# Moving the depthwise convolution of 128 channels from TensorE and VectorE to GpSimd, in the mixing layers of a two-block transformer on one Trainium2 core

## The chip, the core and the metric

The kernel runs on one core of one Trainium2 chip. The core has a matrix engine (TensorE, PE in the profile), three engines for elementwise work (VectorE or DVE, ScalarE or ACT, GpSimd or POOL) and a queue that issues transfers (SyncE, SP). Each engine takes its instructions strictly in the order in which they stand in its own queue. An instruction that has to wait for another engine holds up everything behind it in its queue.

The metric is device time in microseconds (us) for one execution of the whole program. Before the change the median of three runs is 1859.77 us.

## What is computed

Two blocks are run over 256 tokens of width 1024, all in float32. The first block has two layers of feed-forward, attention and feed-forward again. The second block has two layers, each a mixing layer and a feed-forward layer with a short convolution. The change touches only the mixing layers. Cut to what matters here, a mixing layer is:

```python
h = rms_norm_2(x, norm_mix_pre[l])
za, zq, zkv, zg, zc, zd = split(h @ w_in[l])
y_conv = conformer_conv(za, ...)     # 256 channels
y_nsa  = nsa_attention(zq, zkv, zg, ...)   # 4 heads, three branches
y_sgu  = spatial_gating(zc, ...)
y_pool = multiscale_pool(zd, ...)
y = concatenate([y_conv, y_nsa, y_sgu, y_pool], axis=-1) @ w_out[l]
x = x + rms_norm_2(y, norm_mix_post[l])

def conformer_conv(z, w, b, ln_g, ln_b):
    a, gate = split(z, 2, axis=-1)
    y = causal_dwconv(a * sigmoid(gate), w, b)   # 31 taps, one weight per channel and tap
    return silu(layer_norm(y, ln_g, ln_b))
```

The convolution is depthwise: each of the 256 channels is a sum of 31 shifted copies of itself, each multiplied with that channel's weight for the tap.

## The kernel before

Activations lie with channels on the 128 partitions and the 256 tokens along a row, so the 256 channels of the convolution are two tiles of 128x256 each. The gated input is `ci` (two tiles, each with 30 zeros ahead for the causal shift), the sums are `yc[0]` and `yc[1]`. All of these, with the attention's probabilities `PP` and their transposes `PT`, are parts of one large tile, `ar`, and carry that name in the profile.

Weights are streamed from HBM in chunks (`wraw`). Each unit of 128x1024 is split into a rounded part and a rest: ScalarE writes `whi`, VectorE writes `wlo` as `wraw` minus `whi`. A product of float32 accuracy then takes three matmuls, which the profile shows as `hh,whi`, `hl,whi`, `hh,wlo` (input side) or `oh,whi`, `ol,whi`, `oh,wlo` (output side, where `oh` and `ol` are the split result of the four parts). Such triples make up nearly all of TensorE's work.

`mix` (one call per layer) records the instructions. `begin` makes the first two column groups, whose outputs are gated by `gated_input` on ScalarE and VectorE. Then the column groups follow in the order of `MIX_ORDER`. Smaller pieces of work are Python generators that are advanced between the matmuls: `conv_gen`, `sgu_gen`, `pool_gen`, `nsa_cmp`, and `nsa_heads` once for each pair of heads. The second `nsa_heads` starts after the first has written its last product, since both use `PP` and `PT`. Last come the 192 matmuls with `w_out`, 48 for each of the four parts in the order of `MIX_ROWS`: spatial gating (2), pooling (3), convolution (0), attention (1). A part's matmuls are recorded when its result has been stored.

Where a generator's instructions land among the matmuls is decided when the program is built, by `Clock`: it adds up an estimated duration for every instruction on every engine, and `on(engine, ...)` lets a generator go on only when its inputs would be ready by then. An engine's prices are the functions handed to `Engine`. For GpSimd that price was 200 ns and 1 ns per column. VectorE's taps of the convolution are a filler: `conv_gen` records them when VectorE is estimated to be less than 1000 ns (`CONV_BEHIND`) behind TensorE, and `fill_gap` when VectorE would sit idle over 400 ns.

The convolution is divided like this. `yc[0]` is 31 taps on VectorE: one `TENSOR_SCALAR` and 30 `SCALAR_TENSOR_TENSOR`, each of which multiplies and adds in one instruction. Of `yc[1]`, the first 18 taps (`NDIAG`) are matmuls in float32 with a diagonal matrix each, `conv` in `MIX_ORDER`, and the other 13 are on VectorE, with one more addition that joins the two. The 18 diagonal matrices are made by ScalarE in `mix_ahead`, during the feed-forward layer before. Then `conv_gen` transposes both sums on TensorE, takes mean and variance on VectorE (`bs`, `mv`, `rs`, `rz`), normalises (`cz`), transposes back, applies Silu on ScalarE (`cs`) and splits into `oh` and `ol`.

Of the kernel before, what the change touches and what calls it, by code (L numbers as in the profile page):

```python
# [32 lines left out]
S = 256  # L33
# [23 lines left out]
MIX_ORDER = 'v u conv cvf kk cw1 q cvt zd'.split()  # L57
# [10 lines left out]
def _weights(seg):  # L68
# [34 lines left out]
    elif kind == "mix":  # L103
        for which in ["ag0", "ag1"] + [w for w in MIX_ORDER if w != "conv"]:
            n = 1 if which in ("cvf", "kk") else 2
            out.append((("cw1", l) if which == "cw1" else ("mixt" if which in ("v", "cvt", "zd") else "mix", l, which), n))
# [270 lines left out]
NDIAG = 18  # L377
# [55 lines left out]
class Clock:  # L433
# [6 lines left out]
    def __init__(self, nc):  # L440
# [25 lines left out]
        self.gpsimd = Engine(nc.gpsimd, self, "pool", lambda op, out, *a: 200 + size(out))  # L466
# [198 lines left out]
class K:  # L665
# [1103 lines left out]
    def conv_gen(self, l, ci, ready, y, products):  # L1769

        nc = self.nc
        taps = [0, NDIAG]

        def tap():
            t = int(ready[1] and taps[1] <= taps[0])
            if taps[t] == 31:
                t = 1 - t
            if taps[t] == 31 or t and not ready[1]:
                return False
            j = taps[t]  # L1780
            taps[t] += 1
            w = self.v("cw", (l * 2 + t) * 31 + j)
            if j == t * NDIAG:
                nc.vector.tensor_scalar(y[t], ci[:, t, j:j + S], w, self.v("cb", l * 2 + t),
                                        op0=OP.mult, op1=OP.add)
            else:
                nc.vector.scalar_tensor_tensor(y[t], ci[:, t, j:j + S], w, y[t], op0=OP.mult, op1=OP.add)
            return True

        while min(taps) < 31:  # L1790
# [251 lines left out]
    def mix_ahead(self, l):  # L2042
# [22 lines left out]
        self.diags = [self.ar[:, AR - 128 * i - 128:AR - 128 * i] for i in range(NDIAG)]  # L2065
        for j, d in enumerate(self.diags):
            yield from self.on("act", out=[d])
            nc.scalar.activation(d, self.c("ident"), AF.Copy, scale=self.v("cw", (l * 2 + 1) * 31 + j))
            yield
        self.there = l  # L2070

    def mix(self, l, norm, following):
# [14 lines left out]
        assert AR - 128 * NDIAG >= self.ar_at - 2687  # L2087
# [18 lines left out]
        def gated_input(t, ps):  # L2106
# [8 lines left out]
            if t == 0:  # L2115
                self.fillers.append(store(self.conv_gen(l, ci, gated, yc, convp), 0))
# [4 lines left out]
        convp = []  # L2121

        def conv_products():

            self.wait(lambda: gated[1])
            ps = self.mm()
# [198 lines left out]
```

## Time and profile before

| | |
|---|---|
| median of three runs | 1859.77 us (1859.73 to 1861.74) |
| the profiled execution | 1859.25 us, of which its span is 1857.5 us |
| PE busy | 1791.3 us (96%) |
| VectorE busy | 1478.0 us (80%) |
| ScalarE busy | 1006.7 us (54%) |
| GpSimd busy | 42.8 us (2%), 51 instructions |
| first mixing layer | from about 1226 to 1331 us of the span |
| second mixing layer | from about 1544 to 1649 us of the span |

Busy time on PE is the sum of matmuls that overlap in a pipeline, so 96% says that the engine seldom stands still and not that it is at its peak. The two mixing layers run the same program and make up some 11% of the span; everything that the change removes or adds, but for the diagonal matrices, lies in them. Within a mixing layer the profile is read by stretches, since its first part (the column groups) and its second (the two pairs of heads, one after the other) wait for different things. Nearly every row has the same source line, that of the helper which records instructions, so instructions are told apart by the names of their tiles.

### The profile page before, as it was taken

The numbers are of one execution on the slowest core, as the hardware profiler recorded it, in microseconds if no ns is written. First come the engines' busy times: TensorE is split into PE (matmuls) and PEld (weight loads), VectorE is DVE, ScalarE is ACT, GpSimd is POOL, SyncE is SP. The second block draws the span as 40 slices with busy tenths as digits, with TensorE's granted clock in tenths as the row PEclk, the third lists the DMA queues.
The fourth block names the chain that finished last, engine by engine and source line by source line (L and its number), as shares of the span: only waits on it lengthen the run. The fifth ranks groups of instructions, "written<-read, shape, count | busy, mean of one in ns | idle before, by whom it ended". The sixth has DMA issues, their size and how long they took to land.

```text
span 1857.5 us, 36497 instructions
## 1 busy us (share of the span) xinstructions
PE 1791.3 (96%) x15134; PEld 1749.9 (94%) x15134; DVE 1478.0 (80%) x2694; ACT 1006.7 (54%) x1705; POOL 42.8 (2%) x51
## 2 busy tenths in 40 slices
PE   6999999999999999999999999999899999999997
PEld 6999998999999999999999899998799998889997
DVE  6978798898779867779788865589698879869876
ACT  3534568544454445555565654454676554567653
POOL 0200010000000000000000000000000000000000
PEclk9999999999999999999999999999999999999999
DMA  9799374499849873533433566533256533325550
GB/s 383 308 342 341 125 294 184 144 367 351 316 151 345 338 272 134 182 137 123 145 119 137 205 246 221 187 130 137 92 198 215 185 146 136 114 78 206 216 182 24
DMA packets 54471, 378.86 MB, mean 204 GB/s; under 512 B 6304, under 2 KB 7808, under 8 KB 9376
## 3 DMA queue, kind: packets, MB, share of 16 engines
q1 hardware_dynamic: 52992, 372.94, 54.3%
q0 software_dynamic: 1168, 3.46, 0.6%
q8 instruction: 118, 1.93, 0.4%
q14 instruction: 49, 0.40, 0.1%
q10 hardware_dynamic: 144, 0.13, 0.0%
HBM read 375.41 MB, written 1.05 MB: 203 GB/s over the span
## 4 chain that ended last, share of the span: by engine, by line
PE 69%; issue 18%; DVE 7%; ACT 5%; POOL 1%; DMA 0%; POOLq 0%; SPq 0%; DVEq 0%; ACTq 0%
PE banks L427 69%; DVE wlo L427 2%; DVE ar L427 2%; ACT ar L427 2%; ACT whi L427 1%; POOL rz L427 1%; DVE x L427 1%; ACT L427 1%; ACT hh L427 1%; DVE sq L427 0%; DVE hl L427 0%; DMA x<-x 0%; ACT sq L427 0%; DVE ht L427 0%; DVE rs L427 0%
## 5 line engine op out<-in xcount | busy, mean ns | idle before, releaser
L427 DVE TENSOR_TENSOR wlo<-wraw,whi 128x1024 fp32r<-128x1024 f32 x557 | 669.7, 1220 | 172.2 <-ACT whi L427 171.2
L427 PE MATMUL banks<-hh,whi 128*128 128x256 f32 (+1 forms) x2792 | 796.2, 285 | 7.6 <-ACT hh L427 4.7
L427 PE MATMUL banks<-hh,wlo 128*128 128x256 f32 (+1 forms) x2792 | 786.1, 282 | 2.2 <-DVE wlo L427 2.2
L427 PE MATMUL banks<-hl,whi 128*128 128x256 f32 (+1 forms) x2792 | 786.2, 282 | 0.2
L427 ACT CAST whi<-wraw 128x1024 fp32r<-128x1024 f32 x557 | 569.6, 1048 | 172.2 <-DMA wraw<-w 85.1
L427 PEld LDWEIGHTS banks<-hh,whi 128*128 128x128 f32 x2792 | 529.3, 190 | 11.2 <-ACT hh L427 5.6
L427 PEld LDWEIGHTS banks<-hh,wlo 128*128 128x128 f32 x2792 | 529.2, 190 | 2.9 <-DVE wlo L427 2.9
L427 PEld LDWEIGHTS banks<-hl,whi 128*128 128x128 f32 x2792 | 530.0, 190 | 1.1 <-DVE hl L427 1.1
L427 PE MATMUL banks<-oh,whi 128*128 128x256 f32 x1312 | 373.1, 284 | 9.1 <-ACT oh L427 4.3
L427 PE MATMUL banks<-ol,whi 128*128 128x256 f32 x1312 | 368.7, 281 | 4.0 <-DVE ol L427 3.8
L427 PE MATMUL banks<-oh,wlo 128*128 128x256 f32 x1312 | 368.1, 281 | 0.0
L427 PEld LDWEIGHTS banks<-oh,whi 128*128 128x128 f32 x1312 | 247.6, 189 | 16.9 <-ACT oh L427 5.6
L427 PEld LDWEIGHTS banks<-ol,whi 128*128 128x128 f32 x1312 | 247.8, 189 | 4.9 <-DVE ol L427 4.9
L427 PEld LDWEIGHTS banks<-oh,wlo 128*128 128x128 f32 x1312 | 247.7, 189 | 0.0
L427 DVE CUSTOM_DVE_ANT_0 wraw<-wraw,cb 128x1024 f32<-128x1024 f32 x128 | 152.0, 1216 | 0.4 <-DMA wraw<-w 0.4
L427 ACT ACTIVATE sg<-banks 128x256 f32<-128x256 f32 x82 | 31.4, 384 | 176.2 <-PE banks L427 176.1
L427 PE MATMUL banks<-whi,hh 128*128 128x256 f32 x352 | 103.0, 293 | 1.6 <-ACT hh L427 1.4
L427 PE MATMUL banks<-whi,hl 128*128 128x256 f32 x352 | 99.6, 283 | 0.0
L427 PE MATMUL banks<-wlo,hh 128*128 128x256 f32 x352 | 99.3, 282 | 0.0
L427 DVE SCALAR_TENSOR_TENSOR cy<-cs,vec,cy 128x255 f32<-128x255 f32 (+1 forms) x176 | 83.6, 480 | 7.8 <-ACT cy L427 4.7
L427 DVE TENSOR_TENSOR sg<-banks,sg 128x256 f32<-128x256 f32 x82 | 34.4, 422 | 66.1 <-ACT sg L427 66.1
L427 ACT ACTIVATE cy<-cs,vec 128x256 f32<-128x256 f32 x88 | 47.9, 594 | 49.6 <-DVE cs L427 48.8
(207 smaller groups left out, 1698.8 us busy)
## 6 DMA issues: line engine op xcount, KB each, us to landing
wraw<-w SPq DMA_DIRECT2D x342, 1024.0 KB, 4.9
ar<-w SPq DMA_DIRECT2D x8, 1024.0 KB, 10.5
wraw<-w SPq DMA_DIRECT2D x5, 512.0 KB, 3.2
ar<-lw POOLq DMA_DIRECT2D x2, 752.0 KB, 4.8
x<-x SPq DMA_DIRECT2D x1, 1024.0 KB, 6.6
out<-x SPq DMA_DIRECT2D x8, 128.0 KB, 1.9
ar<-bands POOLq DMA_DIRECT2D x1, 544.0 KB, 8.3
cb<-c SPq DMA_DIRECT2D x1, 512.0 KB, 4.5
```

Of the source, the lines that this page charges most:

```text
L427: return f(out, *args, **kw)
```

## The change

The second 128 channels are summed on GpSimd alone. For each tap GpSimd multiplies the shifted row into one half of a new tile `ctmp`, and adds that half to `yc[1]`: 31 multiplications (the first adds the bias and writes `yc[1]` itself) and 30 additions of 128x256 for each layer. The 18 matmuls, VectorE's 13 taps and its joining addition go, and so do the diagonal matrices. A zeroing of 128x960 columns (`blk`, read by `cvf`) goes from GpSimd to VectorE. GpSimd's price in `Clock` is raised to 200 ns and 1.5 ns per column, 2.1 for an operation on two tensors. `conv_gen` waits for a third entry in `gated`, which is appended when the last addition has been recorded. The core of the diff:

```diff
-MIX_ORDER = 'v u conv cvf kk cw1 q cvt zd'.split()
+MIX_ORDER = 'v u cvf kk cw1 q cvt zd'.split()
...
-        self.gpsimd = Engine(nc.gpsimd, self, "pool", lambda op, out, *a: 200 + size(out))
+        self.gpsimd = Engine(nc.gpsimd, self, "pool", lambda op, out, *a: 200 + (2.1 if op == "tensor_tensor" else 1.5) * size(out))
...
-        while not products:
+        while len(ready) < 3:
             yield
-        yield from self.on("dve", products[0])
-        nc.vector.tensor_tensor(y[1], y[1], products[0][:, :S], op=OP.add)
-        self.rel(products[0])
         yield from self.on("pe", *y)
...
-        self.diags = [self.ar[:, AR - 128 * i - 128:AR - 128 * i] for i in range(NDIAG)]
-        for j, d in enumerate(self.diags):
-            yield from self.on("act", out=[d])
-            nc.scalar.activation(d, self.c("ident"), AF.Copy, scale=self.v("cw", (l * 2 + 1) * 31 + j))
-            yield
...
+        tmp = v3(self.qkt("ctmp"))
 
         def conv_products():
 
-            self.wait(lambda: gated[1])
-            ps = self.mm()
-            for j, d in enumerate(self.diags):
-                nc.tensor.matmul(ps[:, :S], d, ci[:, 1, j:j + S], start=j == 0, stop=j == NDIAG - 1)
-                if j % 3 == 2:
-                    self.step()
-            convp.append(ps)
-
+            for j in range(31):
+                while not gated[1] or nc.behind("pool") > CONV_BEHIND:
+                    yield
+                src, w = ci[:, 1, j:j + S], self.v("cw", (l * 2 + 1) * 31 + j)
+                if j == 0:
+                    nc.gpsimd.tensor_scalar(yc[1], src, w, self.v("cb", l * 2 + 1), op0=OP.mult, op1=OP.add)
+                else:
+                    nc.gpsimd.tensor_scalar(tmp[:, j % 2], src, w, None, op0=OP.mult)
+                    nc.gpsimd.tensor_tensor(yc[1], yc[1], tmp[:, j % 2], op=OP.add)
+            gated.append(True)
+
+        self.gens.append(conv_products())
...
-            nc.gpsimd.memset(blk, 0.0)
+            nc.vector.memset(blk, 0.0)
```

In `conv_gen` only the 31 taps of `yc[0]` are left for VectorE. Since `Clock` decides the places anew, more rows move than the diff names. Three places follow, all in the first mixing layer; the second has the same rows.

GpSimd's queue at the start of the layer (`rz` is the inverse root of the mean square, `ar` stands here for `ci`, `yc[1]` and `blk`), before:

```order
L427 DMA cb<-turn 128x512
L427 MEMSET ar 128x2x30
L427 TENSOR_TENSOR rz<-var,half 128x2
L427 MEMSET ar 128x960
L427 TENSOR_TENSOR rz<-var,half 128x2 x3
```

and now:

```order
L426 DMA cb<-turn 128x512
L426 MEMSET ar 128x2x30
L426 TENSOR_TENSOR rz<-var,half 128x2
L426 TENSOR_SCALAR ar<-ar,vec 128x256
L426 TENSOR_SCALAR ctmp<-ar,vec 128x256
L426 TENSOR_TENSOR ar<-ar,ctmp 128x256
```

The last two rows come 30 times, and the next `rz` stands behind them all. Each addition waits for a semaphore that the multiplication ahead of it raises.

TensorE's queue around the second pair of heads: `cst,ar` rows are transposes (of probabilities, or of `yc`), `cst,cz` the transposes back of the normalised convolution, `ar` rows alone the products of probabilities and values. Before:

```order
L427 MATMUL banks<-oh,wlo 128x256
L427 MATMUL banks<-cst,ar 128x128 x6
L427 MATMUL banks<-cst,ar 15x128 x2
L427 MATMUL banks<-cst,ar 128x128 x6
L427 MATMUL banks<-cst,ar 15x128 x2
L427 MATMUL banks<-ar 64x256 x2
L427 MATMUL banks<-ar 64x128 x2
L427 MATMUL banks<-ar 64x256 x2
L427 MATMUL banks<-ar 64x128 x2
L427 MATMUL banks<-ar 64x256 x2
L427 MATMUL banks<-oh,whi 128x256
```

and now:

```order
L426 MATMUL banks<-oh,wlo 128x256
L426 MATMUL banks<-cst,ar 128x128 x10
L426 MATMUL banks<-cst,ar 15x128 x2
L426 MATMUL banks<-cst,ar 128x128 x6
L426 MATMUL banks<-cst,ar 15x128 x2
L426 MATMUL banks<-cst,cz 128x128 x4
L426 MATMUL banks<-ar 64x256 x2
L426 MATMUL banks<-ar 64x128 x2
L426 MATMUL banks<-ar 64x256 x2
L426 MATMUL banks<-ar 64x128 x2
L426 MATMUL banks<-ar 64x256 x2
L426 MATMUL banks<-oh,whi 128x256
```

The four transposes of `yc` and the four of `cz`, which stood before the logits of this pair, now stand among its transposes. Ahead of the piece, between this pair's last logits and its first transpose, stood 78 matmuls of `w_out` (30 of the pooling part and the convolution's 48); now there are 24. Behind the piece stood 48 (attention); now there are 96 (convolution, then attention).

VectorE's queue ahead of the convolution's mean and variance (`BN_STATS bs<-banks`), with the reciprocal and the multiplications `ar<-ar,cf` that normalise a pair of heads. Before, for the first pair:

```order
L427 SCALAR_TENSOR_TENSOR ar<-ar,vec 128x256 x9
L427 TENSOR_TENSOR ar<-ar,banks 128x256
L427 TENSOR_TENSOR wlo<-wraw,whi 128x1024
L427 COPY zt<-banks 128x512
L427 RECIPROCAL cf<-sums 128x12
L427 TENSOR_TENSOR cf<-cf,ar 128x6 x2
L427 TENSOR_SCALAR ar<-ar,cf 128x15 x2
L427 TENSOR_TENSOR ar<-ar,cf 128x2x128
L427 TENSOR_TENSOR ar<-ar,cf 128x2x256
```

and now, for the second pair:

```order
L426 SCALAR_TENSOR_TENSOR ar<-ar,vec 128x256 x7
L426 TENSOR_TENSOR wlo<-wraw,whi 128x1024
L426 RECIPROCAL cf<-sums 128x12
L426 TENSOR_TENSOR cf<-cf,ar 128x6 x2
L426 TENSOR_SCALAR ar<-ar,cf 128x15 x2
L426 TENSOR_TENSOR ar<-ar,cf 128x2x128
L426 TENSOR_TENSOR ar<-ar,cf 128x2x256
L426 TENSOR_SCALAR ar<-ar,cf 128x15 x2
L426 TENSOR_TENSOR ar<-ar,cf 128x2x128
L426 TENSOR_TENSOR ar<-ar,cf 128x2x256
L426 BN_STATS bs<-banks 128x6
```

The convolution's mean and variance, which came behind the first pair's normalisation, now come behind the second's. Of the 31 taps of `yc[0]`, 7 stand ahead of the first pair's masks and 24 behind; before, 26 of them and nine of the other 13 taps stood ahead, and nine taps behind. On ScalarE the Silu (`cs`), with the loading of its table, stood between the two pairs' exponentials, which made a second loading of the exponentials' table necessary; now it stands behind the copies of the second pair's transposes, and one loading is gone.

## Rows read from the trace of the kernel before

**Rows 1.** Stretch, length; busy us (x) PE, PEld, DVE, ACT, POOL; PEclk, DMA, GB/s.

```profile
1243.20:1282.00 38.80, 38.33 (x319) 35.22 (x320) 36.85 (x76) 15.94 (x26) 0.00 (x0) 1.00 0.55 212
1282.00:1308.00 26.00, 22.39 (x198) 19.75 (x198) 18.98 (x70) 16.20 (x44) 0.00 (x0) 1.00 0.23 82
1308.00:1331.00 23.00, 22.48 (x186) 20.28 (x184) 14.40 (x47) 15.80 (x43) 0.00 (x0) 1.00 0.39 137
```

**Rows 2.** Chain of waits from 1282 to 1331 us, its shares by line.

```profile
by line: ACT ar L427 22.2%; PE banks L427 16.0%; ACT whi L427 9.7%; DVE ar L427 8.5%; DVE wlo L427 8.0%; ACT L427 7.9%; issue 5.7%; DVE sq L427 4.1%; ACT oh L427 2.6%; DVE rs L427 2.5%; DVE ol L427 2.3%; ACT cs L427 2.1%; DVE cz L427 2.0%; 
```

**Rows 3.** PE in order of time: start, duration, instruction, count [idle before, releaser].

```profile
1248.00 1.46 PE L427 MATMUL banks<-ar 128*128 128x256 f32 x6
...
1250.46 6.75 PE L427 MATMUL banks<-ar 128*128 128x256 f32 x30
```

**Rows 4.** Groups of instructions, shapes kept apart: busy us, mean ns, idle before.

```profile
L427 DVE TENSOR_TENSOR wlo<-wraw,whi 128x1024 fp32r<-128x1024 f32 x557 | 669.7, 1220 | 172.2 <-ACT whi L427 171.2 <-PE banks L427 0.6
...
L427 DVE SCALAR_TENSOR_TENSOR ar<-ar,vec 128x256 f32<-128x256 f32 x84 | 37.1, 481 | 1.0
...
L427 POOL TENSOR_TENSOR rz<-var,half 128x2 f32<-128x2 f32 x14 | 18.6, 1325 | 1627.6 <-DVE var L427 1627.6
...
L427 ACT ACTIVATE ar<-cst,vec 128x128 f32<-128x128 f32 x36 | 12.7, 396 | 0.0
```

**Rows 5.** VectorE in order of time: the gated input, and taps of the convolution.

```profile
1242.43 0.75 DVE L427 SCALAR_TENSOR_TENSOR ar<-sg,gy 128x256 f32<-128x256 f32 x2
...
1256.17 5.16 DVE L427 SCALAR_TENSOR_TENSOR ar<-ar,vec 128x256 f32<-128x256 f32 x10
...
1269.29 3.25 DVE L427 SCALAR_TENSOR_TENSOR ar<-ar,vec 128x256 f32<-128x256 f32 x8
```

**Rows 6.** GpSimd in order of time.

```profile
1228.74 1.58 POOL L427 TENSOR_TENSOR rz<-var,half 128x2 f32<-128x2 f32 x1 [82.67 <-DVE var L427]
1230.28 0.89 POOL L427 MEMSET ar<- 128x960 f32 x1
...
1332.97 0.69 POOL L427 TENSOR_TENSOR rz<-var,half 128x2 f32<-128x2 f32 x1 [101.81 <-DVE var L427]
```

**Rows 7.** VectorE beside those two GpSimd operations.

```profile
1228.43 0.16 DVE L427 TENSOR_SCALAR var<-banks 128x2 f32<-128x2 f32 x1 [0.96 <-PE banks L427]
1228.52 2.36 DVE L427 TENSOR_TENSOR wlo<-wraw,whi 128x1024 fp32r<-128x1024 f32 x2
...
1332.81 0.86 DVE L427 TENSOR_SCALAR ar<-banks,vec 128x256 f32<-128x256 f32 x2
```

**Rows 8.** PE in order of time: convolution's transposes back, second logits, last triples.

```profile
1302.90 0.60 PE L427 MATMUL banks<-cst,cz 128*128 128x128 f32 x4
...
1307.19 0.93 PE L427 MATMUL banks<-kr,qr 64*128 64x128 f32 x8 [0.94 <-ACT cs L427]
...
1330.20 0.28 PE L427 MATMUL banks<-oh,whi 128*128 128x256 f32 x1
...
1330.79 0.28 PE L427 MATMUL banks<-oh,wlo 128*128 128x256 f32 x1
```

**Rows 9.** VectorE: from the convolution's statistics to its normalisation; second normalisation's end.

```profile
1295.14 0.43 DVE L427 BATCH_NORM_STATS2 bs<-banks 128x6 f32<-128x256 f32 x1
...
1298.11 0.99 DVE L427 TENSOR_SCALAR cz<-banks,mv,rz 128x256 f32<-128x256 f32 x2
...
1320.12 1.02 DVE L427 TENSOR_TENSOR ar<-ar,cf 128x256 f32<-128x256 f32 x2
```

**Rows 10.** ScalarE: Silu, its split, and the table loaded again.

```profile
1306.12 1.02 ACT L427 ACTIVATE cs<-banks,vec 128x256 f32<-128x256 f32 x2
1307.17 0.62 ACT L427 CAST oh<-cs 128x512 fp32r<-128x512 f32 x1
...
1309.98 1.28 ACT L427 ACT_TABLE_LOAD   x1
```

**Rows 11.** A stretch behind the layer's last matmuls, columns as in rows 1.

```profile
1334.00:1339.00 5.00, 3.35 (x13) 2.77 (x14) 3.81 (x10) 2.05 (x4) 0.00 (x0) 0.50 0.01 2
```

More of the change, by code (lines that the diff above doesn't have):

```diff
@@ L103, in _weights @@
     elif kind == "mix":
-        for which in ["ag0", "ag1"] + [w for w in MIX_ORDER if w != "conv"]:
+        for which in ["ag0", "ag1"] + MIX_ORDER:
             n = 1 if which in ("cvf", "kk") else 2
@@ L370, in _host_bands @@
     return np.ascontiguousarray(np.concatenate(out, axis=1), np.float32)
-NDIAG = 18
 CONV_BEHIND = 1000
@@ L1767, in mean_var, with conv_gen @@
         return mv, self.rsqrt(v, n)
-    def conv_gen(self, l, ci, ready, y, products):
+    def conv_gen(self, l, ci, ready, y):
         nc = self.nc
-        taps = [0, NDIAG]
+        count = 0
         def tap():
[L1775 to L1778, printed above, removed]
-                return False
[L1780 to L1785, printed above, removed]
+            nonlocal count
+            if count == 31:
+                return False
+            j, w = count, self.v("cw", l * 62 + count)
+            count += 1
+            if j == 0:
+                nc.vector.tensor_scalar(y[0], ci[:, 0, j:j + S], w, self.v("cb", l * 2), op0=OP.mult, op1=OP.add)
             else:
-                nc.vector.scalar_tensor_tensor(y[t], ci[:, t, j:j + S], w, y[t], op0=OP.mult, op1=OP.add)
+                nc.vector.scalar_tensor_tensor(y[0], ci[:, 0, j:j + S], w, y[0], op0=OP.mult, op1=OP.add)
             return True
-        while min(taps) < 31:
+        while count < 31:
             nc.filler = None
@@ L2086, in mix @@
         self.PT = self.ar_t(2048)
-        assert AR - 128 * NDIAG >= self.ar_at - 2687
         self.busy, self.logits, self.turn = set(), 0, 0
@@ L2115, in gated_input @@
             if t == 0:
-                self.fillers.append(store(self.conv_gen(l, ci, gated, yc, convp), 0))
+                self.fillers.append(store(self.conv_gen(l, ci, gated, yc), 0))
         first = self.begin(norm, [("mix", l, "ag0"), ("mix", l, "ag1")])
@@ L2120, in mix @@
             self.gens.append(gated_input(t, first[t]))
-        convp = []
+        tmp = v3(self.qkt("ctmp"))
         def conv_products():
-            self.wait(lambda: gated[1])
-            ps = self.mm()
-            for j, d in enumerate(self.diags):
-                nc.tensor.matmul(ps[:, :S], d, ci[:, 1, j:j + S], start=j == 0, stop=j == NDIAG - 1)
-                if j % 3 == 2:
-                    self.step()
-            convp.append(ps)
+            for j in range(31):
+                while not gated[1] or nc.behind("pool") > CONV_BEHIND:
+                    yield
+                src, w = ci[:, 1, j:j + S], self.v("cw", (l * 2 + 1) * 31 + j)
+                if j == 0:
+                    nc.gpsimd.tensor_scalar(yc[1], src, w, self.v("cb", l * 2 + 1), op0=OP.mult, op1=OP.add)
[4 more added lines that the diff above has]
+        self.gens.append(conv_products())
         u = [None]
@@ L2214, in zd @@
             self.gens.append(store(self.pool_gen(l, zt), 3))
-        f = {"v": v_, "u": u_, "conv": conv_products, "cvf": cvf, "kk": kk, "cw1": cw1, "cvt": cvt, "q": q_, "zd": zd}
+        f = {"v": v_, "u": u_, "cvf": cvf, "kk": kk, "cw1": cw1, "cvt": cvt, "q": q_, "zd": zd}
         heads()
```

## The prediction

> **What bounds the kernel now.** I read the busy time of each engine by stretches first, then the chain of waits in the stretch where TensorE has gaps, and then single operations in order of time. The two mixing layers run the same rows, so I work one out and double it. The reader is to see that a mixing layer has two halves with different bounds. Up to 1282 us TensorE is busy for 38.3 of 38.8 us and VectorE for 36.9 [rows 1]: both are full, and what is taken from TensorE here can be gained only if VectorE keeps up. From 1282 us on TensorE has gaps (22.4 of 26.0 us) and VectorE has room (19.0 of 26.0, then 14.4 of 23.0) [rows 1]. There the chain runs through the attention: ScalarE's exponentials and copies `ar` hold 22% of it, TensorE's matmuls 16% [rows 2]. The two pairs of heads follow one another, and TensorE's matmuls with `w_out` fill the time in which their softmax is under way.
>
> **What is removed.** On TensorE 18 taps are 36 rows, since a float32 product shows as two: 1.46 + 6.75 = 8.2 us for a layer [rows 3]. They stand in the full half, on the path. On VectorE 13 taps and one addition go. A tap lasts 0.48 us [rows 4]; ten in a row on the same sum take 5.16 us, 0.52 each, while eight that alternate between two sums take 3.25, 0.41 each [rows 5]. What goes are alternating ones, and what is left all adds to one sum: 44 taps at 18 x 0.52 + 26 x 0.41 = 20.0 us become 31 x 0.52 = 16.1, a relief of about 4 us with the addition, not 7. The zeroing of 960 columns that VectorE takes over lasted 0.89 us on GpSimd [rows 6]; some 3 us remain. ScalarE makes 18 diagonal matrices less, 18 x 0.396 = 7.1 us [rows 4], but in the feed-forward layer before, where nothing waits for them; I cost that at nothing. One loading of a table, 1.28 us [rows 10], is gone ahead of the second exponentials. The second logits waited 0.94 us for `cs` [rows 8]; the convolution's late work is gone from there too.
>
> **What GpSimd needs.** The trace of before has no multiplication or addition of 128x256 on GpSimd. The nearest rows bound it. A zeroing, which reads nothing, takes 0.89 us for 960 columns [rows 6], so 0.24 for 256. With one such pass for each tensor read, the multiplication is at least 0.24 and the addition 0.48: 0.24 + 30 x 0.72 = 22 us. An operation on two columns took 0.69 us [rows 6]; with all of that as a fixed part on top, they are 0.93 and 1.17: 64 us. I take the middle, 43 us; the changed planner's own prices, 0.584 and 0.738 us, give 40. The input is gated at 1242.43 + 0.75 = 1243.2 us [rows 5], so left alone GpSimd would be done at 1286, and between 1265 and 1307 by the bounds.
>
> **Whether it is left alone.** It is not, by the one GpSimd operation that the trace repeats. `rz` takes 0.69 us when VectorE reads from PSUM beside it, and 1.58 when VectorE computes `wlo` from two operands in SBUF [rows 6, 7]; its 14 instances (mean 1.325 us [rows 4]) fall into these two kinds, four and ten. In the long ones `rz` ends at 1230.32, and the first of the two `wlo` at 1228.52 + 1.22 = 1229.74 [rows 4, 6, 7]. So GpSimd was held until VectorE's instruction had ended, and came in ahead of the next. Nearly all that VectorE does while GpSimd would sum has two operands in SBUF. In the new order there are 17 `wlo` and 30 taps with two operands between the gated input and the second pair's reciprocal, 17 x 1.22 + 30 x 0.48 = 35 us [rows 4], beside smaller ones. A GpSimd instruction also has parts in which it doesn't read; I take it that it reads for 0.6 of its time, between 1 (each `wlo` costs its whole length) and 0 (nothing). That holds it up by 0.6 x 35 = 21 us: `yc[1]` is complete at 1286 + 21 = 1307.
>
> VectorE should wait in turn. With 43/61 = 0.70 us for a GpSimd instruction, of which 0.42 reading, one of VectorE's 47 instructions meets a read 0.6 of the time and waits half of it: 47 x 0.6 x 0.21 = 6 us. Its bounds are 0 (with two columns the second `wlo` shows no delay: 2.36 us for the two [rows 7]) and 47 x 0.42 = 20 us. The first half has no slack on VectorE to take this up, as 4 - 1 = 3 us of relief stand against 8.2 on TensorE, so I put the 6 us on the path whole.
>
> *By the Trainium skill* ("SBUF — State Buffer", section "Who interferes with whom") the two engines share a port that is locked for a whole instruction, and the loser fully blocks; a VectorE instruction with two SBUF inputs contends with a GpSimd one that reads. The ten long `rz` agree for GpSimd's side; VectorE's side no row here shows. By that, all 35 us would be added, `yc[1]` would be complete at 1321, and the sum below would come to about 1880 us.
>
> **Where it ends.** Before, the second normalisation ended at 1320.12 + 1.02 = 1321.1 us [rows 9]. It comes earlier by 8.2 + 0.94 + 1.28 = 10.4, and later by 6: 1316.7. The convolution's statistics now stand behind it on VectorE, and `yc[1]` at 1307 is in time for them. From statistics to `cz` takes 1298.11 + 0.99 - 1295.14 = 4.0 us [rows 9], the transposes back 0.60 [rows 8], Silu 1.02 and the rounding 0.62 [rows 10], with four handovers at 0.15 (from the end of `var` to the start of `rz` [rows 6, 7]): 1316.7 + 6.8 = 1323.5. Only then can the convolution's 48 matmuls start, and the attention's 48 stand behind them. A matmul comes every (1330.79 - 1330.20) / 5 = 0.118 us [rows 8]: 96 x 0.118 = 11.3 us, so the layer's last starts its successor at 1334.8, against 1330.9 before. That is **3.9 us later**, although TensorE has 8.2 us less to do: the convolution's matmuls no longer fill the second softmax (24 instead of 78 there, 54 x 0.118 = 6.4 us of cover lost), and its normalisation, which lay beside the first pair of heads, lies at the end of everything.
>
> TensorE will stand still for some 5 us or more at that softmax. Behind gaps at the layer's end the granted clock fell to 0.50 over 5 us [rows 11], which is the lower of its two levels, 1.2 of 2.4 GHz; gaps of under 2 us in the second half left it at 1.00 [rows 1]. A stretch of 5 us at half the clock costs 2.5; I take half of that, 1.3 us, between 0 and 2.5.
>
> **The sum.** 2 x (3.9 + 1.3) = 10.4 us on the profiled execution's 1859.25 us, of which 1857.5 are its span: 1869.7. The median of the runs is 0.5 above the profiled execution, so I say 1870 us, 0.55% slower.
>
> **The rivals.**
>
> *The ports don't hold anyone.* If GpSimd's long operations get through beside VectorE, the 6 us go: 3.9 - 6 = -2.1 us a layer, and with the clock's 0 to 1.3 the whole comes to 1855 to 1858. For it speaks that only two columns were ever seen to wait; against it, that all ten did. This is the case of no change, at its lower end just faster.
>
> *TensorE's time is simply saved.* 2 x 8.2 = 16.4 us: 1843. That asks for a second half in which TensorE sets the pace. The chain there speaks against it [rows 2], as does the new order, which puts 96 matmuls behind the last normalisation. It decides if the planner's places turn out not to bind.
>
> *GpSimd itself ends last.* With 64 us, the upper price, and 21 us of holding, `yc[1]` is complete at 1328. TensorE then waits at its transposes, with the second pair's transposes behind them in the queue, and from there it is 0.6 + 0.15 for these, 6.8 and 11.3 to the end: 1347, which is 16 us later, 17.4 with the clock: 1859.25 + 35 = 1894. It decides from `yc[1]` later than about 1316. This is a slower case of its own, dearer than mine.
>
> *The change doesn't move the convolution:* it does, by the order of the instructions; no chance is left for that.
>
> **How the numbers follow.** My forecast, ports that hold and a late tail, 1862 to 1885: 0.52. GpSimd last, 1885 to 1900: 0.17. No holding, 1855 to 1858: 0.23, of which 0.06 below the line of 0.2% that a measurement of this kernel can tell from no change (3.7 us). TensorE's time saved: 0.08. Faster is then 0.14; within 0.2% 0.17 and a margin from the lower end of my own case, 0.19; slower 0.67. The range leaves out the case that TensorE's time is saved and the uppermost of the case in which GpSimd ends last: 1854 to 1896.
>
> **What would show it.** GpSimd's 122 operations of 128x256 with their mean: 0.58 and 0.74 us if nothing holds them, well over 1 us beside `wlo` if the ports do. `wlo` and the taps longer than 1.22 and 0.48 us would show that VectorE is held too. A gap on TensorE of some 5 us between the second logits and its next transposes, then `w_out`'s 96 matmuls in one piece at the layer's end, would show the lost cover; the row that ends the gap says whether `yc` (GpSimd) or the second normalisation (VectorE) came last. The granted clock behind that gap shows the last term. I am wrong if VectorE's rows keep their lengths, or if the stretch up to the first logits shrinks by 8 us and nothing is given back behind it.

## The result, and the profile after

The changed kernel takes 1874.4 us (median of four runs, 1874.1 to 1876.3), beside 1860.8 us for the kernel before on the same chip: 1.0076 times as long, with a 95% interval of 1.0064 to 1.0088. The profiled execution is the slowest of the four, 1876.25 us with a span of 1874.3. It is 17.0 us longer than the profiled one of before, so its rows show some 3 us more than the medians do.

First the groups of instructions that are new or changed, as in [rows 4] (busy us, mean ns, idle before). The helper's line is 426 now.

```profile
L426 DVE TENSOR_TENSOR wlo<-wraw,whi 128x1024 fp32r<-128x1024 f32 x557 | 675.2, 1230 | 166.8 <-ACT whi L426 166.5
...
L426 POOL TENSOR_SCALAR ctmp<-ar,vec 128x256 f32<-128x256 f32 x60 | 80.2, 1336 | 0.0
...
L426 POOL TENSOR_TENSOR ar<-ar,ctmp 128x256 f32<-128x256 f32 x60 | 55.2, 920 | 5.0
...
L426 DVE SCALAR_TENSOR_TENSOR ar<-ar,vec 128x256 f32<-128x256 f32 x60 | 39.5, 658 | 1.4
```

GpSimd's multiplication lasts 1.34 us and its addition 0.92 us in the mean. A tap on VectorE has grown from 0.48 to 0.66 us, and `wlo` from 1.220 to 1.230 in the mean of the whole kernel. Where `wlo` lies beside GpSimd it is up to 1.76 us.

Then the stretches that answer to [rows 1] (columns as there; everything lies 0.6 us later than before by the start of this layer).

```profile
1243.80:1282.00 38.20, 37.45 (x346) 35.10 (x345) 36.83 (x79) 21.52 (x50) 36.65 (x32) 1.00 0.59 220
1282.00:1308.00 26.00, 19.82 (x156) 16.83 (x155) 21.06 (x40) 10.75 (x22) 25.00 (x24) 0.93 0.32 119
1308.00:1340.00 32.00, 24.27 (x168) 20.69 (x166) 21.18 (x62) 14.98 (x40) 6.24 (x7) 0.79 0.19 66
```

In the first half TensorE and VectorE are as full as before. The first logits come at 1275.39 us instead of 1281.88 (before, then after):

```profile
1281.88 1.58 PE L427 MATMUL banks<-kr,qr 64*128 64x128 f32 x16
...
1275.39 1.58 PE L426 MATMUL banks<-kr,qr 64*128 64x128 f32 x16
```

By the layer's own start that is 7.1 us earlier, most of the 8.2 that TensorE was spared. They are lost behind the first logits, most of them in the last stretch, in which TensorE works for 24 of 32 us at a granted clock of 0.79. What it waits for shows in order of time, first on PE, then on VectorE (its last line is of before) and GpSimd (start, us, instruction, count, [idle before, releaser]); the other rows of before are [rows 8, 9].

```profile
1316.39 1.12 PE L426 MATMUL banks<-cst,ar 128*128 128x128 f32 x4 [5.08 <-DVE ar L426]
1318.69 0.45 PE L426 MATMUL banks<-cst,ar 128*128 128x128 f32 x1 [1.18 <-DVE ar L426]
1319.29 3.43 PE L426 MATMUL banks<-cst,ar 128*128 128x128 f32 x15 [0.15 <-DVE ar L426]
1323.93 1.26 PE L426 MATMUL banks<-cst,cz 128*128 128x128 f32 x4 [1.21 <-DVE cz L426]
...
1328.21 0.38 PE L426 MATMUL banks<-oh,whi 128*128 128x256 f32 x1
```

```profile
1311.83 4.51 DVE L426 SCALAR_TENSOR_TENSOR ar<-ar,vec 128x256 f32<-128x256 f32 x7
1316.26 1.22 DVE L426 TENSOR_TENSOR wlo<-wraw,whi 128x1024 fp32r<-128x1024 f32 x1
1317.39 0.22 DVE L426 RECIPROCAL cf<-sums 128x12 f32<-128x12 f32 x1
...
1319.33 1.02 DVE L426 TENSOR_TENSOR ar<-ar,cf 128x256 f32<-128x256 f32 x2
...
1318.17 0.22 DVE L427 RECIPROCAL cf<-sums 128x12 f32<-128x12 f32 x1
```

```profile
1313.65 0.84 POOL L426 TENSOR_TENSOR ar<-ar,ctmp 128x256 f32<-128x256 f32 x1
```

TensorE stands still for 5.1 us ahead of the convolution's transposes. GpSimd ends `yc[1]` at 1313.65 + 0.84 = 1314.49, but VectorE ends `yc[0]`, its own half, only at 1311.83 + 4.51 = 1316.34, and that ends the wait. Behind these seven taps stands a `wlo`, and behind that the reciprocal of the second softmax, at 1317.39 instead of 1318.17 before. So the attention has lost all but 0.8 us of its lead (1.4 on the layer's own clock), and the convolution's normalisation, its transposes and the 96 matmuls with `w_out` follow in one row, from 1328.21 on.

One row gives each mixing layer as a whole, from the first `sq` that opens it to the `sq` that opens its successor; before, then after (columns as in [rows 1]).

```profile
1225.60:1328.85 103.25, 98.20 (x825) 90.20 (x825) 83.95 (x216) 57.34 (x125) 2.42 (x2) 1.00 0.39 143
...
1542.61:1646.52 103.91, 97.42 (x789) 88.71 (x788) 83.30 (x217) 55.07 (x123) 2.37 (x2) 0.97 0.39 143
```

```profile
1226.21:1337.68 111.47, 96.48 (x790) 87.56 (x789) 92.69 (x203) 56.55 (x124) 69.46 (x62) 0.92 0.37 133
...
1551.64:1662.38 110.74, 94.96 (x761) 85.89 (x760) 91.76 (x204) 54.12 (x122) 70.52 (x62) 0.92 0.37 134
```

The first layer is 8.2 us longer and the second 6.8 (110.74 against 103.91). In each VectorE executes 13 instructions fewer and is busy for over 8 us more (8.7 in the first). Outside the two layers the kernel has grown by less than 2 us: the span is 16.8 us longer in all.

### The profile page after: what moved, and what is told of

It reads as the page before. It is cut to its first block, busy times and chain, and to the rows that moved or that the text cites. A ratio compares the mean times of both kernels' runs of the same rounds, so it can differ in the third digit from the quotient of the medians.

```text
span 1874.3 us, 36401 instructions
## 1 busy us (share of the span) xinstructions
PE 1788.4 (95%) x15062; PEld 1745.9 (93%) x15062; DVE 1496.0 (80%) x2668; ACT 994.9 (53%) x1667; POOL 178.4 (10%) x171
## 5 line engine op out<-in xcount | busy, mean ns | idle before, releaser
L426 POOL TENSOR_TENSOR rz<-var,half 128x2 f32<-128x2 f32 x14 | 18.8, 1345 | 1478.7 <-DVE var L426 1478.7
```

Source lines behind the costliest of these rows:

```text
L426: return f(out, *args, **kw)
```

## The experiments

Medians beside the kernel before on the same chip:

| kernel | us | ratio to before, 95% interval |
|---|---|---|
| after | 1874.4 | 1.0076 (1.0064 to 1.0088) |
| e1, GpSimd only writes | 1867.4 | 1.0034 (1.0021 to 1.0047) |
| e2, gap filled | 1874.9 | 1.0073 (1.0058 to 1.0088) |
| e3, left out | 1856.8 | 0.9979 (0.9969 to 0.9989) |
| e4, thirteen taps | 1863.1 | 1.0009 (1.0000 to 1.0019) |
| e5, not awaited | 1879.8 | 1.0103 (1.0086 to 1.0120) |
| e7, kept apart | 1879.4 | 1.0102 (1.0087 to 1.0117) |
| e6, 16 taps / 20 taps | 1879.0 / 1876.2 | 1.0099 (1.0084 to 1.0114) / 1.0084 (1.0069 to 1.0099) |
| e11, multiplications | 1866.3 | 1.0029 (1.0019 to 1.0039) |
| e12, additions | 1894.3 | 1.0177 (1.0162 to 1.0192) |
| e10, thirteen apart | 1867.5 | 1.0039 (1.0024 to 1.0054) |
| e13, ScalarE's products | 1879.8 | 1.0097 (1.0084 to 1.0114) |

### Is VectorE held, and what does that cost?

**e1** keeps the changed kernel's order and lets GpSimd write without reading.

```diff
-                    nc.gpsimd.tensor_scalar(tmp[:, j % 2], src, w, None, op0=OP.mult)
-                    nc.gpsimd.tensor_tensor(yc[1], yc[1], tmp[:, j % 2], op=OP.add)
...
+                    nc.gpsimd.real.memset(wide[:, :960], 0.0)
...
+                        nc.gpsimd.real.memset(wide[:, :740], 0.0)
```

> The changed kernel in the same order, but GpSimd's 61 instructions per mixing layer only write zeros, on tiles sized to last about as long (960 and 740 columns); the convolution of the second 128 channels is left out. GpSimd then reads nothing from SBUF while VectorE works. Theory (VectorE is held by GpSimd's reads): VectorE's taps fall back from 0.66 to about 0.48 us and wlo from 1.23 to 1.22, some 8 us of VectorE time per layer; the five microseconds' gap of TensorE behind the second logits shrinks to 1 to 2 us, and the kernel comes to 1858 to 1864 us. Rival (only the order and the lost cover behind the second softmax cost, the holding is beside the path): rows of VectorE may shorten, but the time stays above 1870 us.

```profile
L426 DVE TENSOR_TENSOR wlo<-wraw,whi 128x1024 fp32r<-128x1024 f32 x557 | 670.0, 1220 | 175.1 <-ACT whi L426 174.8
...
L426 DVE SCALAR_TENSOR_TENSOR ar<-ar,vec 128x256 f32<-128x256 f32 x60 | 28.9, 482 | 1.4
```

```profile
1225.86:1332.31 106.45, 94.97 (x790) 86.69 (x790) 82.76 (x204) 56.65 (x124) 49.77 (x62) 0.95 0.38 139
...
1546.35:1656.13 109.78, 96.88 (x760) 86.96 (x760) 82.61 (x203) 54.07 (x122) 49.80 (x62) 0.89 0.36 135
```

PE's wait, and the end of the second normalisation on VectorE:

```profile
1312.11 1.12 PE L426 MATMUL banks<-cst,ar 128*128 128x128 f32 x4 [3.63 <-DVE ar L426]
```

```profile
1315.05 1.02 DVE L426 TENSOR_TENSOR ar<-ar,cf 128x256 f32<-128x256 f32 x2
```

VectorE's rows are back at 1.220 and 0.482 us: writing does not hold it, reading does. VectorE has 92.69 - 82.76 = 9.9 us less to do in the first layer, for the same instructions in the same order. But the kernel gains only 7.0 us in all, between what the two expectations said, and a wait of 3.6 us for VectorE's own last taps stays. In this order the holding explains half of the 13.6 us lost against before; the other half is what the new order costs beyond what the removed work saves.

**e3** asks what the change would give if GpSimd's work were free: only the zeroing of its result is left.

```diff
-            for j in range(31):
...
+            while not gated[1]:
+                yield
+            nc.gpsimd.memset(yc[1], 0.0)
             gated.append(True)
```

> The changed kernel without the convolution of the second 128 channels: GpSimd only zeroes its result once. This is the price of everything but GpSimd's work: TensorE 8.2 us less, 44 taps become 31, nothing held. Theory (late tail and lost cover remain): the second logits come about 10 us earlier than before the change, the end of the layer 2 to 5 us earlier, 1850 to 1856 us. Rival (TensorE's time is simply saved once nothing holds): 2 x 8.2 us less than before, 1843 us or under. Rival (the loss is all order): 1865 us or more.

```profile
1225.83:1327.26 101.43, 92.36 (x790) 85.37 (x789) 80.47 (x203) 57.53 (x125) 1.83 (x2) 0.98 0.40 146
```

The kernel takes 1856.8 us, some 4 us less than before and 0.8 above the range of the first theory. Leaving the 18 taps out of TensorE and 13 taps out of VectorE, with nothing in their place, is worth no more than 2 us per layer. The rival of 1843 us falls, whatever GpSimd does.

The late tail of that theory is gone too, since in e3 the planner also laid the work out otherwise: `yc[0]` is complete at 1294 us and the convolution's normalisation lies ahead of the second softmax, at 1301, so that `w_out`'s matmuls fill it. Why is the normalisation late in the changed kernel? The planner accounts for SBUF by pieces of 512 bytes (`GRAIN`). `yc[0]` lies at columns 3676 to 3931 of `ar`, and a piece is 128 columns. So it shares its first piece with the end of `ci`, which GpSimd reads, and its last with the beginning of `yc[1]`, which GpSimd writes. By the code the planner then takes VectorE's taps to wait for GpSimd by turns, and spreads them until the layer's end. On the chip there is no such wait: the seven taps above run one behind the other.

**e5** gives e3 its GpSimd work back, on scratch tiles, with nobody waiting for it.

```diff
             nc.gpsimd.memset(yc[1], 0.0)
+            real = nc.gpsimd.real
+            real.memset(tmp, 0.0)
+            for j in range(31):
+                real.tensor_scalar(tmp[:, 0], ci[:, 1, j:j + S], self.v("cw", (l * 2 + 1) * 31 + j), None, op0=OP.mult)
+                real.tensor_tensor(tmp[:, 1], tmp[:, 1], tmp[:, 0], op=OP.add)
```

> The kernel without the convolution of the second 128 channels (1856.8 us), to which GpSimd's 31 multiplications and additions are given back on scratch tiles whose result nobody reads: VectorE is held as in the changed kernel, in an order that does not wait for GpSimd. With the changed kernel (late, held: 1874.4), the one in which GpSimd only writes (late, not held: 1867.4) and the one without (early, not held: 1856.8) it closes a square. Theory (holding and late order add up, 7.0 us for the holding in both layers): 1862 to 1866 us. Rival (the holding cost 7 us only because the late order waits for VectorE's last taps): 1857 to 1860 us.

```profile
1225.89:1339.36 113.47, 96.44 (x789) 88.25 (x789) 92.91 (x203) 57.73 (x125) 69.74 (x65) 0.92 0.35 131
```

Both expectations fall. With no engine waiting for GpSimd the kernel takes 1879.8 us, 22.9 us more than e3 and 5.3 more than the changed kernel itself. In the first layer VectorE's busy time grows by 92.91 - 80.47 = 12.4 us and the layer by 113.47 - 101.43 = 12.0: in this order every microsecond that VectorE is held is paid. One place shows how (VectorE, then PE, in order of time; first e3, then e5).

```profile
1278.62 7.77 DVE L426 SCALAR_TENSOR_TENSOR ar<-ar,vec 128x256 f32<-128x256 f32 x15
...
1282.85 10.01 DVE L426 SCALAR_TENSOR_TENSOR ar<-ar,vec 128x256 f32<-128x256 f32 x15
...
1293.91 0.68 DVE L426 COPY zt<-banks 128x512 f32<-128x512 f32 x1
1294.52 0.21 DVE L426 RECIPROCAL cf<-sums 128x12 f32<-128x12 f32 x1
```

```profile
1288.18 1.20 PE L426 MATMUL banks<-ar,zt 128*64 128x144 f32 x16 [0.95 <-DVE zt L426]
...
1294.64 1.71 PE L426 MATMUL banks<-ar,zt 128*64 128x144 f32 x12 [7.08 <-DVE zt L426]
```

Fifteen taps take 10.0 us instead of the 7.8 of e3, `zt` and the first reciprocal stand behind them, and TensorE waits for 7.1 us instead of 1.0. The four runs form a square (the normalisation is the convolution's; early is e3's order, late that of the changed kernel):

| | not held | held |
|---|---|---|
| normalisation early | e3 1856.8 | e5 1879.75 |
| normalisation late | e1 1867.4 | after 1874.42 |

The two causes do not add up. The late order costs 10.6 us where nothing is held, and saves 5.3 where VectorE is held. Taps that are spread out to the layer's end may leave VectorE room to be held in; no run tests that reason by itself.

### Which of GpSimd's two instructions does it?

**e11** and **e12** are e5 with 62 multiplications, or 62 additions, in a layer.

```diff
-                real.tensor_tensor(tmp[:, 1], tmp[:, 1], tmp[:, 0], op=OP.add)
+                real.tensor_scalar(tmp[:, 1], ci[:, 1, j:j + S], self.v("cw", (l * 2 + 1) * 31 + j), None, op0=OP.mult)
```

```diff
-                real.tensor_scalar(tmp[:, 0], ci[:, 1, j:j + S], self.v("cw", (l * 2 + 1) * 31 + j), None, op0=OP.mult)
+                real.tensor_tensor(tmp[:, 0], ci[:, 1, j:j + S], tmp[:, 0], op=OP.add)
```

> As the kernel with GpSimd's unread work on scratch tiles (1879.75 us; without any such work 1856.8), but that work is 62 multiplications per layer, each reading one 128x256 tile from SBUF; again without the convolution of the second 128 channels. Theory A (what holds VectorE is the number of GpSimd instructions that read SBUF): about as slow, 1874 to 1884 us. Theory B (it is the operands read: a multiplication reads one tile, an addition two): 62 tiles read instead of 93, two thirds of 22.9 us, 1868 to 1874 us, and the one with additions clearly slower than this one. Theory C (one-tile operations do not hold VectorE): 1857 to 1861 us.

> The same with 62 additions per layer instead, each reading two 128x256 tiles from SBUF; without the convolution of the second 128 channels. Theory A (number of instructions): 1874 to 1884 us, as with multiplications. Theory B (operands read, 124 tiles against 93): 1884 to 1890 us. Theory C: 1879 us and more, since all of the holding would be the additions'.

The layer's row, with multiplications and with additions:

```profile
1227.31:1333.84 106.53, 95.29 (x791) 87.15 (x790) 85.39 (x203) 57.87 (x125) 78.09 (x65) 0.95 0.38 139
```

```profile
1225.93:1346.69 120.76, 99.59 (x791) 91.53 (x790) 99.52 (x204) 57.65 (x125) 59.72 (x65) 0.87 0.34 123
```

None of the three theories fits both. 62 multiplications cost VectorE 85.39 - 80.47 = 4.9 us (0.08 each) and the layer 5.1; 62 additions cost it 99.52 - 80.47 = 19.1 us (0.31 each) and the layer 19.3. An addition holds VectorE four times as much as a multiplication, although it reads only two tiles instead of one and is over sooner. Thirty-one of each should cost half of the two sums, (4.9 + 19.1) / 2 = 12.0 us, and e5 showed 12.4. What happens is seen where a `wlo` meets one of them. VectorE and GpSimd in e11:

```profile
1255.04 1.22 DVE L426 TENSOR_TENSOR wlo<-wraw,whi 128x1024 fp32r<-128x1024 f32 x1
```

```profile
1255.00 1.96 POOL L2118 TENSOR_SCALAR ctmp<-ar,vec 128x256 f32<-128x256 f32 x1
1256.94 0.92 POOL L2117 TENSOR_SCALAR ctmp<-ar,vec 128x256 f32<-128x256 f32 x1
```

and in e12:

```profile
1255.29 1.75 DVE L426 TENSOR_TENSOR wlo<-wraw,whi 128x1024 fp32r<-128x1024 f32 x1
```

```profile
1254.89 1.07 POOL L2117 TENSOR_TENSOR ctmp<-ar,ctmp 128x256 f32<-128x256 f32 x1
1256.04 1.59 POOL L2118 TENSOR_TENSOR ctmp<-ctmp 128x256 f32<-128x256 f32 x1
...
1257.71 0.72 POOL L2117 TENSOR_TENSOR ctmp<-ar,ctmp 128x256 f32<-128x256 f32 x1
```

The multiplication, which is 0.92 us alone, started 0.04 us ahead of `wlo` and gave way: it lasts 1.96 us and `wlo` keeps its 1.22. The addition, 0.72 us alone, did not: `wlo` lasts 1.75, and only the next addition is held in turn, until `wlo` ends at 1257.04. The two pairs are no exceptions. Of the 31 `wlo` in e11 that began while a multiplication was under way, 26 kept their length and none lasts over 1.42 us; the 22 in e12 that began beside an addition last 1.65 to 1.76, all of them. The Trainium skill ("SBUF — State Buffer", section "Who interferes with whom") says that a VectorE instruction with two inputs in SBUF contends with a GpSimd one that reads and not with one that only writes; e1 agrees with that (0.482 us for a tap beside writes). The same section of the Trainium skill says that the order of issue decides who blocks. The two pairs are no test of that, since both GpSimd instructions began while VectorE's `sy`, which reads two tiles too, was still under way (in e11 until 1255.11, first line below). In e11 a `wlo` also came 0.15 us behind a multiplication after VectorE had stood idle: there the multiplication kept its 0.92 us and `wlo` waited, which agrees.

```profile
1254.21 0.90 DVE L426 TENSOR_TENSOR sy<-sy,su 128x512 f32<-128x512 f32 x1
...
1639.90 1.40 DVE L426 TENSOR_TENSOR wlo<-wraw,whi 128x1024 fp32r<-128x1024 f32 x1 [4.86 <-ACT whi L426]
```

```profile
1639.75 0.92 POOL L2118 TENSOR_SCALAR ctmp<-ar,vec 128x256 f32<-128x256 f32 x1
```

So a multiplication does hold a `wlo`, but never by more than 0.20 us, and an addition by 0.43 to 0.54. Why the two differ, no run shows.

### The gap and the clock

**e2** puts 40 transposes of the identity into TensorE's gap.

```diff
         tp = yield from self.bank()
+        for i in range(40):
+            nc.tensor.real.transpose(tp[:, i % 4 * 128:i % 4 * 128 + 128], self.c("ident"), self.c("ident"))
         for c in range(2):
```

> The changed kernel with 40 transposes of the identity added on TensorE, just ahead of the transposes that wait for the convolution, where TensorE stands still for 5 us in each mixing layer. If the granted clock of 0.50 behind that gap has a price, the rows behind it (transposes 3.43 us, matmuls with oh, wlo 3.15 us) go back towards the 2.16 and 2.1 to 2.4 us of before, and the kernel gains 3 to 6 us: 1868 to 1872 us. Rival (what follows the gap is set by VectorE and ScalarE, not by TensorE's clock): 1874 us or more, since the transposes can also lie in the way.

Two stretches, first of after and then of e2:

```profile
1316.00:1321.00 5.00, 3.28 (x13) 2.51 (x14) 4.93 (x16) 0.59 (x1) 0.00 (x0) 0.50 0.48 161
...
1326.00:1331.00 5.00, 5.00 (x41) 4.03 (x38) 2.34 (x3) 2.19 (x4) 0.00 (x0) 0.87 0.00 0
```

```profile
1316.00:1321.00 5.00, 2.23 (x15) 1.63 (x16) 4.92 (x15) 0.87 (x3) 0.00 (x0) 1.00 0.47 139
...
1326.00:1331.00 5.00, 5.00 (x38) 3.77 (x34) 1.95 (x3) 2.22 (x4) 0.00 (x0) 0.77 0.02 3
```

Nothing is gained (1874.9 us). Behind the filled gap the clock is at 1.00 instead of 0.50 (2.4 instead of 1.2 GHz), but TensorE there only waits for VectorE's normalisation (4.9 of 5 us busy in both). The clock falls later, to 0.77 where `w_out`'s matmuls begin, and there TensorE is the bound. The low clock was moved, not removed, so this run shows no price for it in this place.

### Other ways to share the work

**e7** moves two small tiles between the result tiles, so that these share no piece.

```diff
-        yc = [self.ar_t(256) for _ in range(2)]
+        yc = [self.ar_t(256)]
+        gates = v3(self.ar_t(24))
+        vc = self.ar_t(64)[:15]
+        yc.append(self.ar_t(256))
```

> The changed kernel with its two result tiles placed so that they share no 512-byte grain of the planner's account: in the changed kernel the planner makes each tap of VectorE wait for GpSimd's last write to the shared grain, and so spreads yc[0]'s taps to the layer's end. Theory (the late order comes from that account): yc[0] is done by about 1300 us instead of 1316, the convolution's normalisation moves ahead of the second pair's, TensorE waits there for GpSimd's yc[1] at about 1313 instead of for VectorE, and the kernel gains, 1864 to 1871 us. Rival (what GpSimd makes late stays late: with yc[1] at 1313 the second pair's transposes are held up in the queue behind it): 1874 us or more.

VectorE and PE in order of time:

```profile
1315.52 0.43 DVE L426 BATCH_NORM_STATS2 bs<-banks 128x6 f32<-128x256 f32 x1 [1.21 <-PE banks L426]
...
1319.40 0.22 DVE L426 RECIPROCAL cf<-sums 128x12 f32<-128x12 f32 x1
```

```profile
1314.37 1.11 PE L426 MATMUL banks<-cst,ar 128*128 128x128 f32 x4 [5.29 <-DVE ar L426]
```

The normalisation does move ahead of the second reciprocal, but the kernel is 5.0 us slower than after, in the rival's range. It is still VectorE's last taps, and not GpSimd, that end TensorE's wait of 5.3 us, and now the second softmax stands behind the convolution: its reciprocal comes at 1319.40 instead of 1317.39. `yc[0]` was not done by 1300 us, as was expected: its last tap ends at 1314.3, 2 us earlier than in after. The edit undid half of the account alone, since `yc[0]` still shares its first piece with `ci`. A kernel without that either was not run, so that the planner's account makes the order late is argued from the code and from e3, where GpSimd does not read, and not shown.

**e6** shares the taps: 16 (or 20) on GpSimd, 15 (or 11) on VectorE, none on TensorE.

```diff
+NPOOL = 16
-CONV_BEHIND = 1000
+CONV_BEHIND = 5000
...
+        yield from self.on("dve", ready[2])
+        nc.vector.tensor_tensor(y[1], y[1], ready[2], op=OP.add)
...
-            for j in range(31):
+            for j in range(NPOOL):
```

> The convolution of the second 128 channels shared: 16 taps on GpSimd (16 x 2.25 = 36 us held, done at about 1281 us), 15 on VectorE, none on TensorE; tiles apart, the planner given the held prices and allowed to lay VectorE's taps earlier, so that the convolution's normalisation stands among the second logits. Theory (the loss is the late order plus some 0.18 us for each tap that meets GpSimd; TensorE's 8 us are a gain where the order keeps its cover): 1855 to 1861 us. Rival (VectorE, with 46 taps held, becomes the bound of the first half and the normalisation slips late all the same): 1864 us or more.

> The same with 20 taps on GpSimd (45 us, done at about 1289 us) and 11 on VectorE. Theory: VectorE has 4 taps or 2 us less, GpSimd is still done before the second logits: 1854 to 1860 us, and not above the one with 16. Rival: GpSimd's end moves the normalisation, and it is slower than with 16.

The theory's figures are missed by 15 us and more. With 16 taps the rival holds (1879.0 us). With 20 both fail: 1876.2 us is far above the theory, but not slower than with 16, as the rival said. VectorE is held by what GpSimd keeps (a tap lasts 0.54 us in the one with 16) and has 15 or 11 taps more.

**e4** does one part of the change alone: VectorE's 13 taps go to GpSimd and TensorE keeps its 18. **e10** is the same with the tiles apart as in e7.

```diff
+            for j in range(NDIAG, 31):
...
+                    nc.gpsimd.tensor_scalar(tmp[:, j % 2], src, w, None, op0=OP.mult)
+                    nc.gpsimd.tensor_tensor(yc[1], yc[1], tmp[:, j % 2], op=OP.add)
```

> The kernel before with one part of the change alone: the 13 taps of the second 128 channels that were VectorE's are done by GpSimd (a multiplication and an addition each), while TensorE keeps its 18 with the diagonal matrices. GpSimd then needs 13 x 1.73 = 22 us unheld, some 30 held, and is done long before the second softmax. Theory (what costs is VectorE being held, about 0.18 us for each tap that meets GpSimd, against 13 taps of 0.48 saved): VectorE gains 6 us and loses 3 to 4, TensorE loses nothing: 1856 to 1862 us. Rival (each use of GpSimd beside a full VectorE costs on balance): above 1864 us.

> The kernel with VectorE's 13 taps done by GpSimd and TensorE keeping 18 (1863.1 us), with its result tiles apart in the planner's account, so that the convolution's normalisation comes right behind the first logits. Theory (holding is small here, 27 us of GpSimd beside a VectorE that has 6 us less to do; the 2 us lost were the order's): 1857 to 1861 us, the first version not slower than the kernel before. Rival (GpSimd's work costs VectorE what it takes from it, whatever the order): 1862 us or more.

e4 takes 1863.1 us, between its two expectations and at most 0.2% more than before. 13 taps fewer on VectorE are no gain: TensorE is busy for 37.3 of the 38 us from 1244 on and sets the pace of the first half, and VectorE's remaining taps last 0.56 us. With the tiles apart it is 1867.5 us, against the theory. One stretch of the first layer in the profiled executions, of e4 and then of e10:

```profile
1312.00:1322.00 10.00, 10.00 (x91) 9.91 (x91) 6.65 (x33) 9.93 (x30) 0.00 (x0) 1.00 0.29 105
```

```profile
1312.00:1322.00 10.00, 10.00 (x62) 9.86 (x59) 6.12 (x29) 6.65 (x23) 0.00 (x0) 0.63 0.28 105
```

TensorE is busy throughout in both, but e10's granted clock is 0.63 there and 62 matmuls are done instead of 91. Here the clock has a price, (1 - 0.63) x 10 = 3.7 us. It need not be the price of the change: the profiled execution of e10, at 1871.6 us, is 4.0 above the median, and its mean clock is 0.987 where the other three have 0.989. Busy time doesn't explain the fall either, since in the 12 us ahead TensorE was busy for 10.1 us in e10 and 9.6 in e4. Nor is VectorE held more (85.7 us busy in e10's first layer, 86.4 in e4's). So why e10 is slower than e4 in the median stays open.

**e13** was meant to beat the change: ScalarE multiplies, GpSimd only adds.

```diff
-                    nc.gpsimd.tensor_scalar(tmp[:, j % 2], src, w, None, op0=OP.mult)
+                    nc.scalar.activation(tmp[:, j % 2], src, AF.Copy, scale=w)
```

> The changed kernel with the multiplications moved to ScalarE (30 more copies with a scale, some 0.4 us each, in a half in which it is busy for 15 of 38 us); GpSimd only adds, 31 instructions of some 0.74 us instead of 61; tiles apart and VectorE's taps allowed earlier. Theory (the holding goes with GpSimd's time at SBUF): less than half of it is left, GpSimd is done by about 1280 us, and the kernel comes to 1860 to 1870 us, faster than the change. Rival (ScalarE's copies come late for the weights' rounding, and VectorE and TensorE wait for these): 1874 us or more.

It takes 1879.8 us, in the rival's range. VectorE's taps last 0.68 us, longer than the 0.66 of after: what was taken from GpSimd is the half that hardly held VectorE. ScalarE's load counts too. In the changed kernel it was busy for 21.5 of the 38.2 us of the first half, not for the 15 of before that the expectation used. Here TensorE waits 2.5 us for ScalarE's `kp` (0.5 in after), and the first logits come 7.2 us later than in after by the layer's own start. How the loss divides between the two isn't shown. No version that was tried beats the kernel before. e3, with the work left out altogether, gains 4 us; in that order this is all there was to pay GpSimd's company with.

## Why the prediction was right, and where it was not

The side, the place and the range were right: 1870 us was said, 1874.4 came, in a range of 1854 to 1896. Point by point:

- **TensorE's 8.2 us** come out at the first logits: 1281.88 - 1275.39 = 6.5 us earlier, 7.1 by the layer's own start. **VectorE's relief** of some 3 us: e3 shows 83.95 - 80.47 = 3.5.
- **GpSimd's own work**, 43 us between 22 and 64: with 0.92 for a multiplication and 0.73 for an addition beside nothing, 31 x 0.92 + 30 x 0.73 = 50.4 us. Within the bounds, but the two came out the wrong way round: the one that reads a single tile is the dearer.
- **GpSimd held for 21 us**: 69.46 us of GpSimd in the layer, less 1.6 for one `rz`, less 50.4, leaves 17.5, half of the 35 us of VectorE's work that the prediction counted there (it took 0.6 of them). `yc[1]` was complete at 1314.5, not 1307, mostly by the dearer operations. It was not the last to come, so this error cost nothing: VectorE's own taps ended 1.9 us behind it.
- **VectorE held for 6 us** is the term that was mis-sized: it is 9.9 us in the first layer and 9.2 in the second (91.76 against 82.61 in e1). The whole was put on the path; by e1 only 7.0 us of 19 arrive, against the 12 that were put into the sum. So too small a cost and too large a share cancelled in part, and the sum had 5 us too much from this term.
- **The second normalisation 10.4 us earlier** is the step that failed. With no holding at all (e1) its last instruction ends at 1315.05 + 1.02 = 1316.1, 5.3 us earlier than before by the layer's own start. The prediction took all that was removed ahead of it as gained. By the layer's own start e1 leads by 7.5 us at the first logits, 6.0 at the second (1301.43 against 1307.19), 6.3 at the end of the second exponentials (1310.06 against 1316.06) and 5.3 at the reciprocal (1313.11 against 1318.17). So the lead is lost bit by bit. The seven taps and the `wlo` that the new order puts ahead of the reciprocal, which the prediction didn't price, are 0.9 us of it; a `wlo` delayed the reciprocal before as well. With the holding the normalisation ended at 1320.35, where 1316.7 was said (0.6 of that is the layer's later start).
- **From there to the end**: 1316.7 to 1334.8 was said, 18.1 us and 1.3 for the clock; 1320.35 to 1339.73 was measured, 19.4. The normalisation at the end of everything and the 96 matmuls in one piece (11.5 us, 11.3 said) are as described. The granted clock did fall to 0.50 behind the gap, for 10 us instead of 5. No run shows a price for it there, so the term of 1.3 us stays unproven.
- **The sum**: 5.2 us per layer were said; 8.2 and 6.8 were measured in the profiled execution, whose time lies 1.8 us above the median. That the forecast came so near is in part luck: over both layers the sum had 5 us too much for the holding and some 10 us too little for the lead that was lost.

Of the rivals, that GpSimd ends last did not come, though only by 1.9 us. That the ports hold no one falls with e1 (482 against 658 ns for a tap). That TensorE's time is simply saved falls with e3. What the prediction lacked altogether is that GpSimd's two instructions differ: it gave both one share of time at SBUF.

## What to carry to other kernels

Before work goes to an idle GpSimd, look at what VectorE does beside it: where VectorE is full and reads two tiles from SBUF, each 128x256 addition on GpSimd took 0.31 us from it and each multiplication 0.08, together four fifths of the 0.48 us of a tap that VectorE does itself. Price such a move by a run in which the work is left out (here 1856.8 us) and one in which it is done without anyone waiting (here 1879.8): they give what can be gained in that order and the cost of mere company, and neither shows in a list of busy times. And where an order is planned, see whose work it puts ahead of the next wait: here like work on GpSimd cost 7 us in one order and 23 in another, in which VectorE's taps stood ahead of `zt` and of TensorE's wait for it.

## What the hardware showed that was not expected

- On GpSimd a 128x256 multiplication by a number per partition (one tile read) lasts 0.92 us alone and an addition of two tiles 0.72 to 0.73.
- The multiplication mostly gives way to VectorE and the addition does not: 0.08 against 0.31 us lost on VectorE for each, and a `wlo` that began beside one of them lost at most 0.20 us, or 0.43 to 0.54. Why, no run here shows.
- Zeroing 128 x 960 and 128 x 740 two-byte columns, 0.90 and 0.72 us each, left VectorE's taps at 482 ns, the value of before.
